# A two-layer trunk on one core: the upper half of x loaded by blocks and transposed on VectorE instead of TensorE

## The chip, the cores and the metric

The kernel runs on one core of a Trainium2 chip. The metric is the device time of one execution in microseconds; below, the median of three runs and the time of the one execution that was profiled. The core's engines take their instructions in the order in which the program lists them for each engine, and wait for each other by semaphores: TensorE (PE; its weight loads are PEld), VectorE (DVE), ScalarE (ACT), GpSimd (POOL) and SyncE (SP), which issues most of the transfers (DMAs).

## What is computed

Two pre-norm residual layers over 256 positions with 1024 channels, float32: attention with 8 heads of 128 and partial rotary in layer 0, a pooling mixer in layer 1, a squared-ReLU MLP of 4096 behind each, and a last norm. For this change only the front of layer 0 matters:

```python
def rms_norm(x, g):
    xf = x.astype(jnp.float32)
    y = xf * lax.rsqrt(jnp.mean(xf * xf, axis=-1, keepdims=True) + NORM_EPS)
    return (y * g.astype(jnp.float32)).astype(x.dtype)
...
    xn = rms_norm(x, norm_mix[i])
...
    qkv = (xn @ w_qkv).reshape(b, s, 3, N_HEADS, HEAD_DIM)
    q, k, v = [jnp.transpose(qkv[:, :, i], (0, 2, 1, 3)) for i in range(3)]
    q = apply_partial_rope(q, cos, sin)
    k = apply_partial_rope(k, cos, sin)
```

## The kernel before

Every product is a sum of three in a shorter float32 form (float32r): a value is cut into a high part and a low part, and high x high, high x low and low x high are added. For weights, `split_steps` makes the parts: ACT copies a raw slab into `wh` (line 169), then DVE subtracts and writes `wl` (line 173). A slab is 1 MB (128 partitions x 2048 columns). The first two slabs (`raw_v_0`, `raw_v_1`) are cut in four pieces of 512 columns, the others in two of 1024. `pump(n)` puts n such pieces into the program, high then low; `use` makes sure that the pieces needed next are in it. When the last low piece of a slab is in the program, the transfer of the slab three places later is issued on SP (`load_to`, `load`), since there are three raw buffers.

The activations need channels on partitions: x arrives with tokens on partitions (`xt`) and is turned. `transposes(k0, ...)` has PE transpose tile k0 (and its neighbour, n=2) of 128 channels against the identity into PSUM (`tr_a`, line 302); then `evac_h` (ACT, line 308) writes the high part into `xs[:, k, 0:256]`, multiplied by the norm's gain `gcol`, and `evac_l` (DVE, line 314) the low part. The norm's 1/rms is put on later, as a factor of the results.

The stage in question is the loop `for k in range(KT)` at line 471: per tile k of 128 channels, twelve products of 512 columns (line 485) add the tile's share to the four banks `d_v` of v = x w_v (two halves of tokens, two of columns). Slab `v_j` holds the weight rows of tiles 2j and 2j + 1. The dictionary `ahead` says in which step the transposes of later tiles stand. ACT also squares x here (`junk`, line 499), a quarter in each of the steps k = 2 to 5, for the mean square; after step 5 `avar` (DVE), `aerr` (ACT, a square root) and a row of small DVE operations make 1/rms and two diagonal matrices. Behind the loop come k and q of each pair of heads, channel tile by channel tile (`u_k`, `u_q`, lines 375 to 380).

The rotary angles are computed on POOL from `pos_i` and `inv` (`rotary`, lines 437 to 446); DVE takes the last turn (`last_turn`), ACT the sines, POOL the cosine, DVE the tables `ct` and `st`, which every q and k is multiplied with (`qk_evac`, line 557 on).

At the very front PE multiplies zeros (`keep_warm`): six products (N_WARM) before the first transposes, two (N_WARM2) behind them. The zeros are a tile `warm` that DVE sets. The order of all engines is the order of the code (a manual schedule).

Of the kernel before, what the change touches and what calls it, by code (L numbers as in the profile page):

```python
# [11 lines left out]
F32 = mybir.dt.float32  # L12
F32R = mybir.dt.float32r
I32 = mybir.dt.int32
AF = mybir.ActivationFunctionType
# [3 lines left out]
P = 128  # L19
SEQ = 256  # L20
D = 1024
# [18 lines left out]
W_BUFS = 5  # L40
AHEAD = 3
N_WARM = 6
N_WARM2 = 2

# [38 lines left out]
def tile_trunk(ctx: ExitStack, tc: tile.TileContext, x_in, positions, norm_mix, norm_mlp,  # L85
# [16 lines left out]
    def rows(ap, r0):  # L102
        return ap[r0:r0 + 2 * P, :].rearrange("(k p) f -> p k f", p=P)

    def cols(ap, c0):
        return ap[:, c0:c0 + 2 * P].rearrange("(k p) f -> p k f", p=P)

    wv = w_qkv[:, 2 * D:3 * D]
    for j in range(4):
        slabs.append((("v", j), rows(wv, 2 * P * j)))  # L110
    for j in range(4):
        slabs.append((("k", j), cols(w_qkv, D + 2 * P * j)))
        slabs.append((("q", j), cols(w_qkv, 2 * P * j)))
# [25 lines left out]
    def load(i):  # L139
        key, ap = slabs[i]  # L140
        if key[0] == "p":
            raws[i] = folded["w"]
            return None
        raw = rawp.tile([P, SLAB], F32, tag="raw", name="raw_%s_%d" % key)
        raws[i] = raw
        rv = raw.rearrange("p (k f) -> p k f", k=ap.shape[1])
        if i > 0:
            nc.sync.dma_start(rv, ap)
        return rv

# [74 lines left out]
        return (wh.rearrange("p (k f) -> p k f", k=kk), wl.rearrange("p (k f) -> p k f", k=kk))  # L225


    warm = cpool.tile([P, P], F32, name="warm")
    nc.vector.memset(warm, 0.0)
    ident = cpool.tile([P, P], F32, name="ident")  # L230
    make_identity(nc, ident)
    ones = cpool.tile([P, P], F32, name="ones")
# [7 lines left out]
    def load_x(k, n):  # L240
        cs = slice(k * P, (k + n) * P)
        nc.sync.dma_start(xt[:, :, cs], x_v[:, :, cs])
# [8 lines left out]
    load_x(0, 1)  # L251
    nc.scalar.dma_start(grow, norm_mix.rearrange("l (k p) -> (l k) p", p=P))
    pos_i = cpool.tile([ROT, SEQ], I32, name="pos_i")
    nc.scalar.dma_start(pos_i, positions.broadcast_to([ROT, SEQ]))
    inv_b = cpool.tile([ROT, P], F32, name="inv")
    nc.scalar.dma_start(inv_b, consts[0:ROT, C_INV:C_INV + P])
    inv = inv_b[:, 0:1]
    load_v0(nc.sync, 0, 0)
    load_v0(nc.sync, 0, 1)
    load_x(1, 1)  # L260
    nc.sync.dma_start(v0[:, 1, :], v0_src[:, 1, :])
    load_x(2, 2)
    raw1 = rawp.tile([P, SLAB], F32, tag="raw", name="raw_v_1")
    raws[1] = raw1
    state["raw"] = 2
    for k in range(2):
        nc.sync.dma_start(raw1[:, k * D:(k + 1) * D], slabs[1][1][:, k, :])
    tiny = cpool.tile([P, 96], F32, name="tiny")[:, 0:1]
    nc.scalar.activation(tiny, warm[:, 0:1], AF.Sqrt)
    load_x(4, 4)  # L270
    nc.sync.dma_start(grow2, norm_mlp.rearrange("l (k p) -> (l k) p", p=P))
    cst = cpool.tile([P, SLAB], F32, name="cst")[:, 0:C_ALL]
    load_to(RAW_BUFS - 1)

    xs = cpool.tile([P, KT, 2 * SEQ], F32R, name="xs")

# [16 lines left out]
    def transposes(k0, gbase, nm, dtag=None, n=2, t=None, tokens=range(NS)):  # L293


        if t is None and dtag:
            t = ps_d.tile([P, HALF], F32, tag=dtag, name="tr_%s_%d" % (nm, k0))
        elif t is None:
            t = ps_t.tile([P, HALF], F32, tag="t", name="tr_%s_%d" % (nm, k0))
        for a in range(n):  # L300
            for s in tokens:
                nc.tensor.transpose(t[:, a * SEQ + s * P:a * SEQ + (s + 1) * P],
                                    xt[:, s, (k0 + a) * P:(k0 + a + 1) * P], ident)

        def evac_h():
            for a in range(n):
                k = k0 + a
                nc.scalar.activation(xs[:, k, 0:SEQ], t[:, a * SEQ:(a + 1) * SEQ], AF.Copy,
                                     scale=gcol[:, gbase + k:gbase + k + 1])

        def evac_l():
            for a in range(n):
                k = k0 + a
                nc.vector.scalar_tensor_tensor(xs[:, k, SEQ:2 * SEQ], t[:, a * SEQ:(a + 1) * SEQ],
                                               gcol[:, gbase + k:gbase + k + 1],
                                               xs[:, k, 0:SEQ].bitcast(F32),
                                               op0=ALU.mult, op1=ALU.subtract)
        return evac_h, evac_l

    def both(pair):  # L320
        pair[0]()
        pair[1]()
# [145 lines left out]
    nc.vector.tensor_scalar(xs[:, 0, 0:SEQ], t0[:, 0:SEQ], gcol[:, 0:1], None, op0=ALU.mult)  # L468
    lo()
    pump_h(1)  # L470
    ahead = {0: (1, 1), 1: (2, 2), 3: (4, 2), 5: (6, 2)}
    for k in range(KT):
        wh, wl = use("v", k // 2, 99 if k % 2 else (2 if k < 4 else 1))
        ev = transposes(ahead[k][0], 0, "a", n=ahead[k][1]) if 0 < k and k in ahead else None
        steps = [(n, h) for n in range(3) for h in range(2)]
        if k == 0:
            steps.sort(key=lambda nh: nh[1])
        for n, h in steps:
            if k == 0 and (n, h) == (0, 1):
                both(transposes(1, 0, "a", n=1))  # L480
            hs = slice(h * HALF, (h + 1) * HALF)
            for s in range(NS):
                x0 = (SEQ if n == 1 else 0) + s * P
                w = wl if n == 2 else wh
                nc.tensor.matmul(dv[s, h], xs[:, k, x0:x0 + P], w[:, k % 2, hs],  # L485
                                 start=k == 0 and n == 0, stop=k == KT - 1 and n == 2)
        if k < 7:
            pump(2 if k < 3 else 1)
        if k == 2:
            load_to(3)  # L490
            nc.sync.dma_start(cst, consts[:, 0:C_ALL])
        if k == 6:
            gains(grow2, 16)
        if ev is not None:
            both(ev)
        if 2 <= k < 6:
            s, h = GR[k - 2]
            junk = work.tile([P, HALF], F32, tag="junk", name="junk", bufs=1)
            nc.scalar.activation(junk, xt[:, s, h * HALF:(h + 1) * HALF], AF.Square,
                                 scale=1.0 / 32.0, accum_out=acc0[:, h, s:s + 1])  # L500
        if k == 5:
            var0 = small.tile([P, NS], F32, tag="avar", name="avar", bufs=1)
            r0t = small.tile([P, NS], F32, tag="arst", name="arst", bufs=1)
            e0 = small.tile([P, NS], F32, tag="aerr", name="aerr", bufs=1)
            nc.vector.scalar_tensor_tensor(var0, acc0[:, 0, :], EPS, acc0[:, 1, :],
                                           op0=ALU.add, op1=ALU.add)
            nc.scalar.activation(e0, var0, AF.Sqrt)
            pump_h(1)
            nc.vector.reciprocal(r0t, e0)
            nc.vector.tensor_tensor(e0, var0, r0t, op=ALU.mult)  # L510
            nc.vector.tensor_tensor(e0, e0, r0t, op=ALU.mult)
            nc.vector.tensor_scalar(e0, e0, -0.5, 1.5, op0=ALU.mult, op1=ALU.add)
            nc.vector.tensor_tensor(r0t, r0t, e0, op=ALU.mult)
            r0 = [r0t[:, s:s + 1] for s in range(NS)]
            diags = []
            for s in range(NS):
                diag = small.tile([P, P], F32, tag="diag%d" % s, name="diag%d" % s, bufs=1)
                nc.vector.tensor_scalar(diag, ident, r0[s], None, op0=ALU.mult)
                diags.append(diag)
# [606 lines left out]
```

## Time and profile before

| | us |
|---|---|
| median of three runs | 485.59 (485.41 to 486.0) |
| the profiled execution, its own time | 485.4 |
| its span, first to last instruction | 483.4 |
| PE busy | 475.7 |
| DVE busy | 333.6 |
| ACT busy | 253.5 |
| POOL busy | 40.8 |

The span is what the engines' records cover; the time has 2.0 us more around it. The rows that are quoted from the timelines read: start in us from the span's start, busy us, engine, line, operation, what is written and read, number of instructions in a row, and in brackets the idle time of the engine ahead of it with what ended it. In the first 45 us the order of PE is: zeros, transposes, v (until 30.03), the first k (from 30.40), the first q (from 36.24), the second k (from 42.00).

### The profile page before, as it was taken

The numbers are of one execution on the slowest core, as the hardware profiler recorded it, in microseconds if no ns is written. First come the engines' busy times: TensorE is split into PE (matmuls) and PEld (weight loads), VectorE is DVE, ScalarE is ACT, GpSimd is POOL, SyncE is SP. The second block draws the span as 40 slices with busy tenths as digits, with TensorE's granted clock in tenths as the row PEclk, the third lists the DMA queues.
The fourth block names the chain that finished last, engine by engine and source line by source line (L and its number), as shares of the span: only waits on it lengthen the run. The fifth ranks groups of instructions, "written<-read, shape, count | busy, mean of one in ns | idle before, by whom it ended". The sixth has DMA issues, their size and how long they took to land.

```text
span 483.4 us, 6621 instructions
## 1 busy us (share of the span) xinstructions
PE 475.7 (98%) x2622; PEld 415.3 (86%) x2622; DVE 333.6 (69%) x492; ACT 253.5 (52%) x413; POOL 40.8 (8%) x38
## 2 busy tenths in 40 slices
PE   9999999999999999999999999999999999999994
PEld 7889999888888888888888889888888888888884
DVE  4789988855877484848566687678756557484745
ACT  5794655653686372635355554477535436272523
POOL 6920344300000000000000000000000000000000
PEclk9999999999999999999999999999999999999998
DMA  8975644480477757557574570078747472845202
GB/s 281 385 227 199 196 175 129 133 261 1 121 250 238 262 195 284 185 164 219 170 250 144 174 262 1 17 250 288 243 138 264 151 255 95 259 127 222 89 0 87
DMA packets 55982, 89.32 MB, mean 185 GB/s; under 512 B 1584, under 2 KB 44688, under 8 KB 55952
## 3 DMA queue, kind: packets, MB, share of 16 engines
q1 hardware_dynamic: 55536, 88.46, 55.3%
q10 hardware_dynamic: 416, 0.45, 0.3%
q8 instruction: 20, 0.33, 0.3%
q14 instruction: 10, 0.08, 0.0%
HBM read 87.85 MB, written 1.05 MB: 184 GB/s over the span
## 4 chain that ended last, share of the span: by engine, by line
PE 98%; DVE 0%; ACT 0%; issue 0%; ACTq 0%
PE u_m L397 24%; PE u_m L390 13%; PE d_m L366 12%; PE d_m L367 12%; PE d_m L368 12%; PE d_v L485 5%; PE u_q L380 2%; PE u_q L376 2%; PE u_k L376 2%; PE u_k L380 2%; PE u_k L375 2%; PE u_q L375 2%; PE d_o L366 2%; PE d_o L368 2%; PE d_o L367 2%; PE d_p L999 1%
## 5 line engine op out<-in xcount | busy, mean ns | idle before, releaser
L397 PE MATMUL u_m<-xs,wh_u 128*128 128x512 f32 x512 | 122.2, 390 | 0.0
L397 PEld LDWEIGHTS u_m<-xs,wh_u 128*128 128x128 f32 x512 | 94.7, 188 | 18.7
L366 PE MATMUL d_m<-wh_d,hh 128*128 128x512 f32 x252 | 98.1, 389 | 0.0
L368 PE MATMUL d_m<-wh_d,hl 128*128 128x512 f32 x252 | 98.0, 389 | 0.0
L367 PE MATMUL d_m<-wl_d,hh 128*128 128x512 f32 x252 | 98.0, 389 | 0.0
L173 DVE TENSOR_TENSOR wl_d<-raw_d,wh_d 128x1024 fp32r<-128x1024 f32 x64 | 76.2, 1221 | 17.6 <-ACT wh_d L169 17.6
L173 DVE TENSOR_TENSOR wl_u<-raw_u,wh_u 128x1024 fp32r<-128x1024 f32 x64 | 75.7, 1221 | 11.3 <-ACT wh_u L169 11.3
L169 ACT ACTIVATE wh_d<-raw_d 128x1024 fp32r<-128x1024 f32 x64 | 64.9, 1047 | 22.5 <-DMA raw_d<-in_mlp_w_down_dram 22.4
L733 ACT ACTIVATE t<-u_m 128x256 f32<-128x256 f32 x64 | 24.0, 378 | 83.1 <-PE u_m L390 54.5
L169 ACT ACTIVATE wh_u<-raw_u 128x1024 fp32r<-128x1024 f32 x64 | 63.9, 1045 | 6.2 <-DMA raw_u<-in_mlp_w_up_dram 6.2
L390 PEld LDWEIGHTS u_m<-xs,wl_u 128*128 128x128 f32 x512 | 64.1, 191 | 1.5
L390 PE MATMUL u_m<-xs,wl_u 128*128 128x256 f32 x512 | 65.3, 284 | 0.0
L734 DVE TENSOR_TENSOR t<-u_m,t 128x256 f32<-128x256 f32 x64 | 26.5, 422 | 53.7 <-ACT t L733 52.9
L368 PEld LDWEIGHTS d_m<-wh_d,hl 128*128 128x128 f32 x252 | 47.3, 188 | 9.8
L366 PEld LDWEIGHTS d_m<-wh_d,hh 128*128 128x128 f32 x252 | 47.3, 188 | 9.8
L367 PEld LDWEIGHTS d_m<-wl_d,hh 128*128 128x128 f32 x252 | 47.3, 188 | 9.8
L744 ACT ACTIVATE hh<-hf 128x512 fp32r<-128x512 f32 x32 | 20.2, 633 | 45.0 <-DVE hf L743 45.0
L745 DVE TENSOR_TENSOR hl<-hf,hh 128x512 fp32r<-128x512 f32 x32 | 22.2, 693 | 22.5 <-ACT hh L744 22.5
L743 DVE SCALAR_TENSOR_TENSOR hf<-t 128x512 f32<-128x512 f32 x32 | 22.2, 692 | 1.1
L375 PE MATMUL u_q<-xs,wh_q 128*128 128x256 f32 x64 | 18.7, 291 | 0.0
L375 PE MATMUL u_k<-xs,wh_k 128*128 128x256 f32 x64 | 18.5, 289 | 0.0
L380 PE MATMUL u_q<-xs,wh_q 128*128 128x256 f32 x64 | 18.1, 283 | 0.0
(205 smaller groups left out, 582.2 us busy)
## 6 DMA issues: line engine op xcount, KB each, us to landing
raw_u<-in_mlp_w_up_dram SPq DMA_DIRECT2D x32, 1024.0 KB, 6.4
raw_d<-in_mlp_w_down_dram SPq DMA_DIRECT2D x32, 1024.0 KB, 4.9
raw_k<-in_attn_w_qkv_dram SPq DMA_DIRECT2D x4, 1024.0 KB, 5.4
raw_q<-in_attn_w_qkv_dram SPq DMA_DIRECT2D x4, 1024.0 KB, 5.3
raw_o<-in_attn_w_o_dram SPq DMA_DIRECT2D x4, 1024.0 KB, 4.9
raw_v<-in_attn_w_qkv_dram SPq DMA_DIRECT2D x2, 1024.0 KB, 8.2
raw_v<-in_attn_w_qkv_dram SPq DMA_DIRECT2D x3, 512.0 KB, 6.5
pw<-in_pool_w_dram SPq DMA_DIRECT2D x1, 1024.0 KB, 9.2
```

The lines of the kernel that those rows point to most:

```text
L169: nc.scalar.activation(wh[:, sl], src[:, sl], AF.Copy)
L173: nc.vector.tensor_tensor(wl[:, sl], src[:, sl], wh[:, sl].bitcast(F32), op=ALU.subtract)
L366: nc.tensor.matmul(acc, lh, wh, start=first, stop=False)
L367: nc.tensor.matmul(acc, lh, wl, start=False, stop=False)
L368: nc.tensor.matmul(acc, ll, wh, start=False, stop=last)
L375: nc.tensor.matmul(o, w[0][:, k, fs], hi, start=first, stop=False, skip_group_check=True)
L380: nc.tensor.matmul(acc[:, f * SEQ:(f + 1) * SEQ], w[0][:, k, fs], xs[:, k, SEQ:2 * SEQ], start=False, stop=last, skip_group_check=True)
L390: nc.tensor.matmul(acc[:, 0:SEQ], w[1][:, k, f * P:(f + 1) * P], xs[:, k, 0:SEQ], start=first and k == 0, stop=not first and k == KT - 1, ...
L397: nc.tensor.matmul(acc, w[0][:, k, f * P:(f + 1) * P], xs[:, k, :], start=first and k == 0, stop=not first and k == KT - 1, skip_group_che ...
L485: nc.tensor.matmul(dv[s, h], xs[:, k, x0:x0 + P], w[:, k % 2, hs], start=k == 0 and n == 0, stop=k == KT - 1 and n == 2)
L733: nc.scalar.activation(t[:, ts], u[:, SEQ:2 * SEQ], AF.Copy)
L734: nc.vector.tensor_tensor(t[:, ts], u[:, 0:SEQ], t[:, ts], op=ALU.add)
```

## The change

x's channels 512 to 1023 get to `xs` in another way. Four DMAs load them a second time, in blocks: partition 32j + b of `xp` holds token b of each of the eight groups of 32 tokens, columns 128j to 128j + 127 of the upper half. `block_tile(k)` has DVE transpose 32x32 blocks of it (every fourth column), which gives a tile whose partition p is channel 512 + 4p + (k - 4); so the upper rows of all weights of q, k and v are loaded in that order (`upper`), and the gains `gx` too. The gain goes on in an ACT copy from SBUF and a DVE operation, as before from PSUM. The transposes of tiles 4 to 7 on PE are gone. `xt` still gets the upper half, for the squares and the residual, but later. Each k and q slab is loaded by two DMAs. The second row of v's first slab comes in two halves, and step 1 of the loop takes the columns' halves one after the other with the transposes of tiles 2 and 3 between them. `pos_i` and `inv` are loaded on SP's queue, behind `raw_v_1`, instead of ACT's. `warm` is a constant instead of a tile of its own, and N_WARM2 is 3.

```diff
-N_WARM2 = 2
+N_WARM2 = 3
...
+    def upper(ap):
+        return ap[HALF:D, :].rearrange("(p k) f -> p k f", k=4)
...
     for j in range(4):
-        slabs.append((("v", j), rows(wv, 2 * P * j)))
+        slabs.append((("v", j), rows(wv, 2 * P * j) if j < 2 else
+                      upper(wv)[:, 2 * j - 4:2 * j - 2, :]))
...
-        if i > 0:
+        if key[0] in ("k", "q"):
+            c0 = (D if key[0] == "k" else 0) + 2 * P * key[1]
+            nc.sync.dma_start(rv[:, 0:4, :], ap[:, 0:4, :])
+            nc.sync.dma_start(rv[:, 4:8, :], upper(w_qkv[:, c0:c0 + 2 * P]))
+        elif i > 0:
             nc.sync.dma_start(rv, ap)
...
-    warm = cpool.tile([P, P], F32, name="warm")
-    nc.vector.memset(warm, 0.0)
+    warm = nc.const_aps.tensor(0.0, (P, P), F32)
...
-    nc.scalar.dma_start(pos_i, positions.broadcast_to([ROT, SEQ]))
...
-    nc.scalar.dma_start(inv_b, consts[0:ROT, C_INV:C_INV + P])
...
-    nc.sync.dma_start(v0[:, 1, :], v0_src[:, 1, :])
+    load_v0(nc.sync, 1, 0)
+    load_v0(nc.sync, 1, 1)
...
+    nc.sync.dma_start(pos_i, positions.broadcast_to([ROT, SEQ]))
+    nc.sync.dma_start(inv_b, consts[0:ROT, C_INV:C_INV + P])
...
+    xp = cpool.tile([P, D], F32, tag="psb", name="xp")
+    xp_i = xp.rearrange("p (i c) -> p i c", i=8)
+    x_b = x_in.rearrange("(i b) (h j c) -> h j b i c", b=32, j=4, h=2)
+    for j in range(4):
+        nc.sync.dma_start(xp_i[32 * j:32 * j + 32], x_b[1, j])
+    gx = cpool.tile([P, 4], F32, name="gx")
+    nc.sync.dma_start(gx, norm_mix[0:1, HALF:D].rearrange("o (p k) -> (o p) k", k=4))
+    load_to(RAW_BUFS - 1)
     load_x(4, 4)
...
-    load_to(RAW_BUFS - 1)
...
+    def block_tile(k):
+
+        t = work.tile([P, SEQ], F32, tag="Y", name="xb_%d" % k, bufs=4)
+        nc.vector.transpose(t.rearrange("p (i b) -> p i b", b=32),
+                            xp.rearrange("p (i a k) -> p i a k", i=8, k=4)[:, :, :, k - 4])
+        g = gx[:, k - 4:k - 3]
+        nc.scalar.activation(xs[:, k, 0:SEQ], t, AF.Copy, scale=g)
+        nc.vector.scalar_tensor_tensor(xs[:, k, SEQ:2 * SEQ], t, g, xs[:, k, 0:SEQ].bitcast(F32),
+                                       op0=ALU.mult, op1=ALU.subtract)
...
-    ahead = {0: (1, 1), 1: (2, 2), 3: (4, 2), 5: (6, 2)}
+    ahead = {0: (1, 1), 1: (2, 2)}
     for k in range(KT):
         wh, wl = use("v", k // 2, 99 if k % 2 else (2 if k < 4 else 1))
-        ev = transposes(ahead[k][0], 0, "a", n=ahead[k][1]) if 0 < k and k in ahead else None
         steps = [(n, h) for n in range(3) for h in range(2)]
-        if k == 0:
+        if k < 2:
             steps.sort(key=lambda nh: nh[1])
         for n, h in steps:
-            if k == 0 and (n, h) == (0, 1):
-                both(transposes(1, 0, "a", n=1))
+            if k < 2 and (n, h) == (0, 1):
+                both(transposes(*ahead[k][:1], 0, "a", n=ahead[k][1]))
...
-        if ev is not None:
-            both(ev)
         if 2 <= k < 6:
+            block_tile(k + 2)
             s, h = GR[k - 2]
```

What stands where on the engines follows from the order of the code. On DVE, in the steps k = 1 to 5 of the v loop, there stood before (wl_v_j is a piece of slab j's low part, tr_a_4 the transposes of tiles 4 and 5 in PSUM):

```order
L173 TENSOR_TENSOR wl_v_1_209<-raw_v_1_105,wh_v_1_208 128x512 x2
L314 SCALAR_TENSOR_TENSOR xs_115<-tr_a_2_191,gcol_123,xs_115 128x256 x2
L173 TENSOR_TENSOR wl_v_1_209<-raw_v_1_105,wh_v_1_208 128x512 x2
L173 TENSOR_TENSOR wl_v_2_257<-raw_v_2_113,wh_v_2_256 128x1024
L314 SCALAR_TENSOR_TENSOR xs_115<-tr_a_4_239,gcol_123,xs_115 128x256 x2
L173 TENSOR_TENSOR wl_v_2_257<-raw_v_2_113,wh_v_2_256 128x1024
L173 TENSOR_TENSOR wl_v_3_302<-raw_v_3_189,wh_v_3_301 128x1024
L314 SCALAR_TENSOR_TENSOR xs_115<-tr_a_6_284,gcol_123,xs_115 128x256 x2
L505 SCALAR_TENSOR_TENSOR avar_311<-acc0_151 128x2
```

On DVE at the same place of the changed kernel (xb_4 to xb_7 are the transposed tiles):

```order
L331 SCALAR_TENSOR_TENSOR xs_121<-tr_a_2_204,gcol_129,xs_121 128x256 x2
L182 TENSOR_TENSOR wl_v_1_220<-raw_v_1_102,wh_v_1_219 128x512 x4
L340 STREAM_TRANSPOSE xb_4_245<-xp_109 128x256
L344 SCALAR_TENSOR_TENSOR xs_121<-xb_4_245,gx_114,xs_121 128x256
L182 TENSOR_TENSOR wl_v_2_264<-raw_v_2_116,wh_v_2_263 128x1024
L340 STREAM_TRANSPOSE xb_5_267<-xp_109 128x256
L344 SCALAR_TENSOR_TENSOR xs_121<-xb_5_267,gx_114,xs_121 128x256
L182 TENSOR_TENSOR wl_v_2_264<-raw_v_2_116,wh_v_2_263 128x1024
L340 STREAM_TRANSPOSE xb_6_290<-xp_109 128x256
```

Each transpose stands behind the low piece of the step before it; it goes on in this way to xb_7 and avar. On ACT, in the same steps, there stood before (junk is the square of a quarter of x):

```order
L169 ACTIVATE wh_v_2_256<-raw_v_2_113 128x1024
L308 ACTIVATE xs_115<-tr_a_4_239,gcol_123 128x256 x2
L499 ACTIVATE junk_264,acc0_151<-xt_90 128x512
L169 ACTIVATE wh_v_2_256<-raw_v_2_113 128x1024
L499 ACTIVATE junk_282,acc0_151<-xt_90 128x512
L169 ACTIVATE wh_v_3_301<-raw_v_3_189 128x1024
L308 ACTIVATE xs_115<-tr_a_6_284,gcol_123 128x256 x2
```

On ACT at the same place of the changed kernel:

```order
L178 ACTIVATE wh_v_1_219<-raw_v_1_102 128x512 x4
L343 ACTIVATE xs_121<-xb_4_245,gx_114 128x256
L524 ACTIVATE junk_249,acc0_157<-xt_88 128x512
L178 ACTIVATE wh_v_2_263<-raw_v_2_116 128x1024
L343 ACTIVATE xs_121<-xb_5_267,gx_114 128x256
L524 ACTIVATE junk_271,acc0_157<-xt_88 128x512
L178 ACTIVATE wh_v_2_263<-raw_v_2_116 128x1024
L343 ACTIVATE xs_121<-xb_6_290,gx_114 128x256
L524 ACTIVATE junk_294,acc0_157<-xt_88 128x512
L178 ACTIVATE wh_v_3_308<-raw_v_3_196 128x1024
```

The copies into xs, two in a row before, now stand one by one between the high pieces, and read what DVE transposed. On SP's queue, after the change, behind the first columns of x and v's first slab:

```order
L250 DMA xt_88<-in_x_dram 128x2x256
L274 DMA raw_v_1_102<-in_attn_w_qkv_dram 128x1024 x2
L275 DMA pos_i_94<-in_positions_dram 32x256
L276 DMA inv_95<-in_consts_dram 32x128
L284 DMA xp_109<-in_x_dram 32x8x128 x4
L286 DMA gx_114<-in_norm_mix_dram 128x4
L157 DMA raw_v_2_116<-in_attn_w_qkv_dram 128x2x1024
L250 DMA xt_88<-in_x_dram 128x2x512
```

Before, x's upper columns (128x2x512) and the second norm's gains stood between raw_v_1 and raw_v_2, and pos_i and inv on ACT's queue at the very start.

## The prediction

> **What bounds the kernel now.** I read the page first, then the timelines of PE, ACT and DVE over the first 45 us, which is all that the change touches. The page says that the end is set by PE alone:
>
> ```profile
> span 483.4 us, 6621 instructions
> PE 475.7 (98%) x2622; PEld 415.3 (86%) x2622; DVE 333.6 (69%) x492; ACT 253.5 (52%) x413; POOL 40.8 (8%) x38
> PE 98%; DVE 0%; ACT 0%; issue 0%; ACTq 0%
> ```
>
> The chain of waits is 98% PE, so a gap that opens in PE's row of products, or one that closes, goes into the time nearly in full. PE's timeline (start, us, what, count) gives the pace at the front, where the eight channel tiles k = 0 to 7 are multiplied with the v columns:
>
> ```profile
> 8.42 0.63 PE L485 MATMUL d_v<-wl_v,xs 128*128 128x512 f32 x2
> 9.10 0.63 PE L302 MATMUL tr_a<-ident,xt 128*128 128x128 f32 x4
> 9.48 2.08 PE L485 MATMUL d_v<-wh_v,xs 128*128 128x512 f32 x8
> 12.31 1.98 PE L485 MATMUL d_v<-wh_v,xs 128*128 128x512 f32 x8
> 15.04 0.60 PE L302 MATMUL tr_a<-ident,xt 128*128 128x128 f32 x4
> 15.39 2.10 PE L485 MATMUL d_v<-wh_v,xs 128*128 128x512 f32 x8
> 27.15 2.12 PE L485 MATMUL d_v<-wh_v,xs 128*128 128x512 f32 x8
> 30.40 0.36 PE L375 MATMUL u_k<-xs,wh_k 128*128 128x256 f32 x1
> 36.24 0.28 PE L375 MATMUL u_q<-xs,wh_q 128*128 128x256 f32 x1
> 42.00 0.28 PE L375 MATMUL u_k<-xs,wh_k 128*128 128x256 f32 x1
> ```
>
> One tile's twelve products take 15.04 - 12.31 = 2.73 us, 0.228 each. Whatever ACT and DVE must do per tile has to fit into 2.73 us, or PE waits. Tile 7 starts at 27.15, the first k product at 30.40.
>
> **What is removed.** Two groups of four transposes leave PE (tiles 4 and 5 at 15.04, tiles 6 and 7 later): 15.39 - 15.04 = 0.35 each, **-0.70 us** if PE stays the bound. The products of tile 0 end at 8.42 + 2 x 0.228 = 8.88, and PE waits until 9.10 for x's next columns. With row 1 of v's first slab in halves and the transposes of tiles 2 and 3 in the middle of tile 1, that 0.22 goes.
>
> **The product more at the front.**
>
> ```profile
> 4.60 1.06 PE L282 MATMUL warm_up<-warm 128*128 128x128 f32 x4
> 4.83 1.39 ACT L169 ACTIVATE wh_v<-raw_v 128x512 fp32r<-128x512 f32 x2 [1.15 <-DMA raw_v<-in_attn_w_qkv_dram]
> ```
>
> Two products (four rows) take some 0.9 us up to the first v product, one some 0.45. That first product needs wh's first half, ready about 4.83 + 0.70 = 5.53, so 0.45 more lies in a wait as long as PE's front starts earlier, which it may, since the zeros no longer wait for a memset on DVE. Bounds: -0.3 (PE reaches its full clock earlier) to +0.45 (no earlier start). I take 0.
>
> **What the moved transposes make: a loop.** The order of the changed kernel has DVE take, per tile, the low half wl of a v piece, then the block transpose T, then xs's low part; ACT takes the copy of T into xs, a square of x, then the next high half wh. So wh -> wl (needs wh) -> T (behind wl on DVE) -> copy (needs T) -> square -> next wh (behind both on ACT). Before, ACT's copies waited for PE, not for DVE. The prices, from ACT and from DVE:
>
> ```profile
> 10.21 1.15 ACT L169 ACTIVATE wh_v<-raw_v 128x512 fp32r<-128x512 f32 x2 [1.01 <-DMA raw_v<-in_attn_w_qkv_dram]
> 11.27 0.82 ACT L308 ACTIVATE xs<-tr_a,gcol 128x256 fp32r<-128x256 f32 x2
> 15.25 1.06 ACT L169 ACTIVATE wh_v<-raw_v 128x1024 fp32r<-128x1024 f32 x1 [1.52 <-DMA raw_v<-in_attn_w_qkv_dram]
> 16.22 0.82 ACT L308 ACTIVATE xs<-tr_a,gcol 128x256 fp32r<-128x256 f32 x2
> 16.93 0.63 ACT L499 ACTIVATE junk<-xt 128x512 f32<-128x512 f32 x1
> 17.45 0.20 ACT L499 ACTIVATION_READ_ACCUMULATOR junk<-xt 128x1 f32 x1
> 17.55 1.05 ACT L169 ACTIVATE wh_v<-raw_v 128x1024 fp32r<-128x1024 f32 x1
> 21.61 0.84 ACT L308 ACTIVATE xs<-tr_a,gcol 128x256 fp32r<-128x256 f32 x2 [1.45 <-PE tr_a L302]
> 23.58 0.21 ACT L507 ACTIVATE aerr<-avar 128x2 f32<-128x2 f32 x1 [0.53 <-DVE avar L505]
> 23.70 1.04 ACT L169 ACTIVATE wh_v<-raw_v 128x1024 fp32r<-128x1024 f32 x1
> ```
> ```profile
> L173 DVE TENSOR_TENSOR wl_v<-raw_v,wh_v 128x1024 fp32r<-128x1024 f32 x4 | 5.4, 1342 | 2.3 <-ACT wh_v L169 2.3
> L173 DVE TENSOR_TENSOR wl_v<-raw_v,wh_v 128x512 fp32r<-128x512 f32 x6 | 4.1, 725 | 0.9 <-ACT wh_v L169 0.9
> 23.27 0.28 DVE L505 SCALAR_TENSOR_TENSOR avar<-acc 128x2 f32<-128x2 f32 x1
> 28.09 1.22 DVE L173 TENSOR_TENSOR wl_k<-raw_k,wh_k 128x1024 fp32r<-128x1024 f32 x1
> 29.22 0.28 DVE L449 TENSOR_SCALAR rot_b<-rot_a 32x256 f32<-32x256 f32 x1
> 33.84 0.43 DVE L543 SCALAR_TENSOR_TENSOR ct_k<-rb,cos_t 128x256 f32<-128x256 f32 x1 [0.99 <-POOL cos_t L459]
> 34.84 0.40 DVE L544 SCALAR_TENSOR_TENSOR st_q<-rb,sin_t 32x256 f32<-32x256 f32 x1
> 36.52 0.01 DVE L557 LOAD_MASK_SELECT sw_k<-u_k  x1 [1.27 <-ACT vsb L530]
> 39.51 2.34 DVE L173 TENSOR_TENSOR wl_k<-raw_k,wh_k 128x1024 fp32r<-128x1024 f32 x2
> 44.06 0.73 DVE L557 STREAM_SHUFFLE sw_q<-u_q 32x512 f32<-32x512 f32 x1
> ```
>
> wh 1.05; hand-over 0.03 (avar ends at 23.55, aerr starts at 23.58); wl 1.34, of which its end overlaps 0.09 with what follows on DVE (28.09 + 1.22 against 29.22), so 1.25; T; hand-over 0.03; copy 0.36 (16.22 to 16.93 for two); square 0.62 (16.93 to 17.55). No transpose on DVE stands in this trace: its bounds are 0.28 (29.22, 256 columns of 32 partitions) and 0.73 (the shuffle, the one other operation here that moves data between partitions, at twice the columns). I take 0.43, the row at 33.84, which has its size. **Loop: 1.05 + 0.03 + 1.25 + 0.43 + 0.03 + 0.36 + 0.62 = 3.77 us, against PE's 2.73.** About 1 us per tile is lost once the lead is used up.
>
> [...] That both engines keep their order is what closes the loop: the row at 21.61 shows ACT idle for 1.45 us in front of a copy while the wh_v at 23.70 stood behind it. [...]
>
> **The sum.** Tile 1: half 0 from 8.88, six products, 10.25; four transposes, the last ends 0.63 later, 10.88. Then ACT: two copies from 10.91 to 11.62, and only now v's second slab in four pieces, 0.53 apart (10.21 to 11.27 for two), the first ready at 12.24. Tile 2 starts at 12.27, as before (12.31): the 0.22 above is given back here. DVE: four low pieces from 12.27, 3 x 0.635 + 0.725, end 14.90; T of tile 4 from 14.81 to 15.24; copy from 15.27, square from 15.63, wh for tile 4 from 16.25 to 17.30. PE wants tile 4 at 12.27 + 2 x 2.73 = 17.73: in time. Tile 5's wh is ready at 17.30 + 3.77 = 21.07, wanted at 20.46: 0.6 late. Tile 6: 24.84, wanted at 23.8: 1.0 late. For tile 7 the variance stands in the loop too: the square's last read (17.45 + 0.20 is 0.72 after 16.93) instead of 0.62, hand-over 0.03, avar 0.28, hand-over 0.03, aerr 0.12 to the next start: 0.56 more. So tile 7's wh is ready at 24.84 + 3.77 + 0.56 = 29.17, wanted at 27.6; tile 7 starts 2.0 us later than at 27.15.
>
> Behind it on DVE stands an unbroken row from the end of aerr (23.79) to the second low half of k's first slab (29.31): 5.52 us. PE had 1.1 us of slack there (30.40). aerr now ends at 29.17 - 1.04 + 0.09 = 28.22, the row at 33.74, and the first k product starts at 33.8 instead of 30.40: **+3.4 us**. PE alone would be ready at 29.2 + 3.25 = 32.45, so DVE comes last.
>
> After that the pieces keep step with PE: second low half of the next k slab at 41.85 (39.51 + 2.34), 0.15 before PE wants it at 42.00, and both move by 3.4. So nothing more is added and, with PE without a gap after, nothing is won back. The two DMAs in the place of one per k and q slab have the same bytes and rows of the same length; ACT reaches those slabs later than before.
>
> **The queues.** pos_i and inv go from ACT's queue, where they were early, behind v's second slab on SP:
>
> ```profile
> 4.62 0.39 POOL L437 CAST rot_a<-pos_i 32x256 f32<-32x256 int32 x1 [2.92 <-DMA pos_i<-in_positions_dram]
> 24.07 0.74 POOL L446 TENSOR_TENSOR rot_a<-rot_a,rot_b 32x256 f32<-32x256 f32 x1
> grow<-in_norm_mlp_dram SPq DMA_DIRECT2D x1, 8.0 KB, 7.3
> 10.00:15.00 5.00, 5.00 (x23) 4.08 (x22) 3.54 (x7) 3.53 (x8) 4.68 (x5) 1.00 1.04 418
> ```
>
> 8 KB that stood behind large loads took 7.3 us to land, so pos_i lands with the slab ahead of it: its first half is waited for until 10.21, the second is 512 KB at 418 GB/s later, 11.5. POOL's row takes 24.81 - 4.62 = 20.2 us, so it ends at 31.7. DVE wants it right after 33.74: covered, by the delay of the loop alone. x's blocks (xp, 512 KB) come next, at 12.7 to 13.5 (full rate to about half of it); T wants them at 14.81. v's third slab has the same bytes ahead of it as before (xp instead of x's upper columns): 15.25 to about 16, wanted at 16.25. If that cover fails, each us of lateness is one of the sum.
>
> **Total: profiled run 485.4 us (span 483.4, 2.0 around it), close to the median of 485.59; 485.4 + 3.4 = 488.8.** Its own range: T of 0.28 or 0.73 makes -0.6 or +1.2 (four in the path), wl of 1.22 -0.4, the front -0.3 or +0.4: 487.5 to 490.8.
>
> **Rivals.**
> - The loop fits (say T stands ready early, its input there since 13.5): then the edits give their 0.70, and 0.2 at the front: 484.5, **faster**. It needs wh, wl, T, copy and square in 2.73 us; wh and wl alone are 2.3, the copy and the square 0.98, so only a T that doesn't wait for wl would do it, and pos_i would have to be early too. 0.06.
> - POOL becomes the bound: with the loop hidden, DVE's last turn of the angles waits until 31.7 instead of 29.22, the tables end 2.5 later, at 37.7 instead of 35.24 (34.84 + 0.40), and the first rotation, begun at 36.52, begins 1.2 later, and with it the low halves that PE waits for at 42.00: 486.6. 0.08.
> - Loads: xp or the third slab lands 1 to 2 us after T or wh wants it, the loop starts that much later: 490 to 490.8. 0.09.
> - Gains and waits balance within 0.2% (1 us, about what a measurement here can tell from no change), with a short T and slack that I don't see: 485.5. 0.06.
> - The forecast, 0.71.
>
> The range 486.9 to 490.8 holds the forecast, the loads and a part of POOL. Faster 0.06, same 0.07, slower 0.87.
>
> **What would show it.** In the changed profile: idle time of ACT before the xs copy, ended by DVE's xb; idle time of DVE before wl_v, ended by ACT's wh_v; starts of wh_v's pieces 3.8 apart; PE gaps of 0.5 to 1.5 us before tiles 5, 6 and 7 and at the first u_k; u_k at about 33.8. The cast of pos_i at 11.5. The step is wrong if wh_v's pieces come under 3 us apart or PE shows no gap there; the rotary step is wrong if the cast is before 8; and a T far from 0.43 moves the sum by four times the difference.

## The result, and the profile after

The changed kernel takes 492.03 us (median of 4 runs, 491.64 to 492.34) against 485.6 us (4 runs, 485.41 to 486.0) for the kernel before on the same chip: a ratio of **1.0131, 95% interval 1.0117 to 1.0146**, 6.4 us slower. The forecast was 488.8 us with a range up to 490.8: the side was right, the size too small by 3.2 us. The head of the page of the profiled execution (span, busy time of each engine, chain of waits):

```profile
span 489.6 us, 6637 instructions
PE 476.1 (97%) x2616; PEld 413.8 (85%) x2616; DVE 337.1 (69%) x495; ACT 254.0 (52%) x413; POOL 40.1 (8%) x38
PE 91%; DMA 3%; DVE 2%; ACT 1%; SPq 1%; issue 0%; DVEq 0%; ACTq 0%
```

PE's busy time is nearly what it was (475.7 before). The span has grown by 6.2 us, and the chain of waits has pieces that stood at nothing before: DMA 3%, DVE 2%, ACT 1%, SP's queue 1%. PE's timeline shows where (start, us, what, count, and in brackets the idle time ahead with what ended it):

```profile
19.74 2.12 PE L511 MATMUL d_v<-wh_v,xs 128*128 128x512 f32 x8 [1.84 <-ACT wh_v L178]
23.64 2.12 PE L511 MATMUL d_v<-wh_v,xs 128*128 128x512 f32 x8 [0.86 <-ACT wh_v L178]
28.06 2.12 PE L511 MATMUL d_v<-wh_v,xs 128*128 128x512 f32 x8 [1.37 <-ACT wh_v L178]
33.05 2.14 PE L511 MATMUL d_v<-wh_v,xs 128*128 128x512 f32 x8 [1.78 <-ACT wh_v L178]
36.63 0.36 PE L402 MATMUL u_k<-xs,wh_k 128*128 128x256 f32 x1
```

Tiles 4, 5, 6 and 7 each wait for the high half of their weights, 1.84, 0.86, 1.37 and 1.78 us. The first k product starts at 36.63 where it started at 30.40: 6.2 us, the whole difference of the spans. Behind it the engines keep step (the first u_q 5.83 us later, 5.84 before), so all of the loss lies in the first 37 us.

What the high halves waited for, from ACT's timeline:

```profile
13.49 1.15 ACT L178 ACTIVATE wh_v<-raw_v 128x512 fp32r<-128x512 f32 x2 [0.90 <-DMA raw_v<-in_attn_w_qkv_dram]
18.63 1.06 ACT L178 ACTIVATE wh_v<-raw_v 128x1024 fp32r<-128x1024 f32 x1 [1.49 <-DMA raw_v<-in_attn_w_qkv_dram]
21.52 0.51 ACT L343 ACTIVATE xs<-xb,gx 128x256 fp32r<-128x256 f32 x1 [1.83 <-DVE xb L340]
22.55 1.04 ACT L178 ACTIVATE wh_v<-raw_v 128x1024 fp32r<-128x1024 f32 x1
26.97 1.04 ACT L178 ACTIVATE wh_v<-raw_v 128x1024 fp32r<-128x1024 f32 x1
31.96 1.04 ACT L178 ACTIVATE wh_v<-raw_v 128x1024 fp32r<-128x1024 f32 x1
```

The first row is the second half of v's second slab, which itself came late, at 13.5. The next, for tile 4, waited for v's third slab, which came in at 18.6. The other three have no wait of their own: ACT is idle ahead of the *copy* in front of them, until DVE has turned a tile (xb). They start 3.92, 4.42 and 4.99 us apart; PE needs 2.73 per tile. That is the loop of the forecast, and DVE and POOL show why it is longer than the 3.77 (4.33 for the last) that was worked out:

```profile
15.37 0.62 DVE L340 STREAM_TRANSPOSE xb<-xp 128x256 f32<-128x256 f32 x1
19.72 1.23 DVE L182 TENSOR_TENSOR wl_v<-raw_v,wh_v 128x1024 fp32r<-128x1024 f32 x1 [2.67 <-ACT wh_v L178]
20.86 0.62 DVE L340 STREAM_TRANSPOSE xb<-xp 128x256 f32<-128x256 f32 x1
23.62 1.73 DVE L182 TENSOR_TENSOR wl_v<-raw_v,wh_v 128x1024 fp32r<-128x1024 f32 x1 [0.86 <-ACT wh_v L178]
28.04 1.70 DVE L182 TENSOR_TENSOR wl_v<-raw_v,wh_v 128x1024 fp32r<-128x1024 f32 x1 [0.89 <-ACT wh_v L178]
35.11 1.22 DVE L182 TENSOR_TENSOR wl_k<-raw_k,wh_k 128x1024 fp32r<-128x1024 f32 x1
36.33 1.22 DVE L182 TENSOR_TENSOR wl_k<-raw_k,wh_k 128x1024 fp32r<-128x1024 f32 x1
37.46 0.27 DVE L476 TENSOR_SCALAR rot_b<-rot_a 32x256 f32<-32x256 f32 x1
```
```profile
13.72 0.39 POOL L464 CAST rot_a<-pos_i 32x256 f32<-32x256 int32 x1 [12.02 <-DMA pos_i<-in_positions_dram]
23.55 0.72 POOL L473 TENSOR_TENSOR rot_a<-rot_a,rot_b 32x256 f32<-32x256 f32 x1
24.36 1.70 POOL L472 TENSOR_SCALAR rot_b<-rot_b 32x256 f32<-32x256 f32 x1
32.33 0.72 POOL L473 TENSOR_TENSOR rot_a<-rot_a,rot_b 32x256 f32<-32x256 f32 x1
```

The block transpose takes 0.62. The low half wl takes 1.23 once and 1.73 and 1.70 in the next two turns. In those two a POOL operation had begun just before: one at 23.55, over at 24.27, and wl ends at 25.35, 1.08 after that; POOL's next one, begun at 24.36, takes 1.70 where its like at 31.35 takes 0.90. wl is 0.50 and 0.47 us longer there than at 19.72, and POOL's operation 0.80 longer than at 31.35; why was not shown. POOL's row of angles, which before ended at 24.8, now ends at 33.05 and so lies beside the whole loop.

Why the slab came late, from SP's timeline, its waits, and the table by stretches (from:to, length, busy us and instructions of PE, PEld, DVE, ACT, POOL, then granted clock, busy share of the DMA engines, GB/s). First the change:

```profile
10.69 0.35 SPq L286 DMA_DIRECT2D gx<-in_norm_mix_dram  x1
13.49 0.39 SPq L157 DMA_DIRECT2D raw_v<-in_attn_w_qkv_dram  x1
SPq L157 <- DMA raw_v<-in_attn_w_qkv_dram: 2.4, 1, 2.4
11.00:14.00 3.00, 2.95 (x13) 2.00 (x12) 2.08 (x4) 2.10 (x5) 0.28 (x1) 1.00 0.91 152
```

Then the kernel before (the row at 6.48 is the third slab's issue and the fourth's):

```profile
6.48 3.93 SPq L148 DMA_DIRECT2D raw_v<-in_attn_w_qkv_dram  x2
11.00:14.00 3.00, 3.00 (x15) 2.49 (x14) 3.00 (x6) 2.74 (x7) 2.83 (x3) 1.00 1.04 420
```

SP issued the third slab at 13.49, after 2.4 us of waiting for a piece of the *second* slab to land. The DMAs here report on eight semaphores in turn, and each waits for the one eight places ahead: in the change six issues in a row, the four of xp, gx and the third slab, come 0.02 us after that one's last report. By SP's and ACT's order of issue the third slab had been eight places behind the second piece of v's first slab and was issued at 6.48. With six DMAs added ahead of it (one piece more of v's first slab, four for xp, gx) and two moved behind it (x's upper columns, the second norm's gains) it is eight places behind the second half of v's second slab, which landed at 13.47 where it had landed at 11.42 before. In the meantime the DMA engines are 91% busy and move 152 GB/s, where the kernel before moved 420 in the same stretch. Over 3 us that is 0.80 MB less, 1.9 us at the old rate. Not all of it is slow packets: with quick ones, in the run with the blocks to all partitions below, the stretch still moves only 212 GB/s, since the third slab goes out at 11.94 there.

### The profile page after: what moved, and what is told of

The parts are those of the page before. It is cut to its first block, busy times and chain, and to the rows that moved or that the text cites. A ratio compares the mean times of both kernels' runs of the same rounds, so it can differ in the third digit from the quotient of the medians.

```text
span 489.6 us, 6637 instructions
## 1 busy us (share of the span) xinstructions
PE 476.1 (97%) x2616; PEld 413.8 (85%) x2616; DVE 337.1 (69%) x495; ACT 254.0 (52%) x413; POOL 40.1 (8%) x38
## 4 chain that ended last, share of the span: by engine, by line
PE 91%; DMA 3%; DVE 2%; ACT 1%; SPq 1%; issue 0%; DVEq 0%; ACTq 0%
PE u_m L424 24%; PE u_m L417 13%; PE d_m L393 12%; PE d_m L395 12%; PE d_m L394 12%; DMA raw_v<-in_attn_w_qkv_dram 3%; PE u_q L407 2%; PE u_k L407 2%; PE u_q L403 2%; PE u_k L403 2%; PE u_k L402 2%; PE u_q L402 2%; PE d_o L393 2%; PE d_o L395 1%; PE d_o L394 1%; DVE wl_v L182 1%
## 5 line engine op out<-in xcount | busy, mean ns | idle before, releaser
L182 DVE TENSOR_TENSOR wl_u<-raw_u,wh_u 128x1024 fp32r<-128x1024 f32 x64 | 75.7, 1221 | 11.5 <-ACT wh_u L178 11.5
L511 PE MATMUL d_v<-wh_v,xs 128*128 128x512 f32 x64 | 17.2, 406 | 6.3 <-ACT wh_v L178 5.8
L511 PEld LDWEIGHTS d_v<-wh_v,xs 128*128 128x128 f32 x64 | 11.3, 188 | 10.6 <-ACT wh_v L178 8.5
L402 PE MATMUL u_q<-xs,wh_q 128*128 128x256 f32 x64 | 18.7, 291 | 0.0
```

The costliest lines, as they stand in the source:

```text
L182: nc.vector.tensor_tensor(wl[:, sl], src[:, sl], wh[:, sl].bitcast(F32), op=ALU.subtract)
L402: nc.tensor.matmul(o, w[0][:, k, fs], hi, start=first, stop=False, skip_group_check=True)
```

## The experiments

Ten kernels ran. Ratios are against the kernel before on the same chip (485.84 us in the first two batches, 485.75 in the last). Times are medians. Where a run is set against the changed kernel, the two ran on chips whose times of the kernel before differ by up to 0.2 us.

**The front alone.** The kernel before with the zeros, the product more, row 1 of v's first slab in halves, and tile 1's order of the change:

```diff
-N_WARM2 = 2
+N_WARM2 = 3
...
-    nc.sync.dma_start(v0[:, 1, :], v0_src[:, 1, :])
+    load_v0(nc.sync, 1, 0)
+    load_v0(nc.sync, 1, 1)
...
-        if k == 0:
+        if k < 2:
             steps.sort(key=lambda nh: nh[1])
```

> The kernel before with the front of the change alone: constant zeros, one fill-up product more, row 1 of v's first slab in halves, step 1 by halves with the transposes of tiles 2 and 3 in its middle. By the prediction's sum these give nothing: 485.6 us, within 0.3. Rival (they are a gain that the rest of the change hides): up to 0.6 less, 485.0 us; or the later copies of tiles 2 and 3 cost: 486.

Measured: 485.32 us (10 runs), ratio 0.9993 [0.9983, 1.0002]. The front costs and brings nothing that can be told from no change.

**The late positions alone.** The kernel before, with pos_i and inv loaded behind `raw_v_1` on SP:

```diff
-    nc.scalar.dma_start(pos_i, positions.broadcast_to([ROT, SEQ]))
-    nc.scalar.dma_start(inv_b, consts[0:ROT, C_INV:C_INV + P])
...
+    nc.sync.dma_start(pos_i, positions.broadcast_to([ROT, SEQ]))
+    nc.sync.dma_start(inv_b, consts[0:ROT, C_INV:C_INV + P])
```

> The kernel before with pos_i and inv alone moved to the sync queue behind v's second slab. By the second rival of the prediction (angles late, tables late): cast at about 11.6 us, last turn near 31.8, second k product 1.2 us later, 486.8 us, 486.3 to 487.3. If the late angles are hidden: 485.6 us.

Measured: 487.29 us (5 runs), ratio 1.0035 [1.0021, 1.0050], +1.45 us. DVE's timeline has the wait that the forecast priced as a rival, in the first row (the second row's 0.99 stood there before, too):

```profile
32.96 0.28 DVE L449 TENSOR_SCALAR rot_b<-rot_a 32x256 f32<-32x256 f32 x1 [2.37 <-POOL rot_a L446]
37.58 0.42 DVE L543 SCALAR_TENSOR_TENSOR ct_k<-rb,cos_t 128x256 f32<-128x256 f32 x1 [0.99 <-POOL cos_t L459]
```

The last turn comes 3.7 us later than at 29.22, of which 1.45 reach the end. In the changed kernel the same turn (37.46 above) has no wait: there the loop covers it.

**All four turns first.** The changed kernel, with the four block transposes in a row in step 2, so that none stands behind a low half of v:

```diff
-    def block_tile(k):
+    xbs = {}
+    def block_turn(k):
         t = work.tile([P, SEQ], F32, tag="Y", name="xb_%d" % k, bufs=4)
+        xbs[k] = t
...
+    def block_tile(k):
+        t = xbs[k]
...
+        if k == 2:
+            for kk in range(4, KT):
+                block_turn(kk)
         if 2 <= k < 6:
```

> The changed kernel with the four block transposes in one row on VectorE in step 2; copies, squares and loads stay. Loop theory (ScalarE and VectorE wait for each other once per tile because each transpose stands behind a wl): the PE gaps before tiles 5, 6 and 7 (1.0, 1.5 and 1.8 us) go, the one before tile 4 (2.0) stays, tile 7 starts near 28.1 instead of 33.05; the late angles on GpSimd (done at 33.05) then take back about 1.2 us: 487.9 us, 487 to 489. Rival (the loads alone make tiles 4 to 7 late): the gaps stay, 491.5 to 492.5 us.

Measured: 489.62 us (9 runs, 486.39 to 490.16), ratio 1.0063 [1.0044, 1.0082]; 2.4 us less than the change. The loop is gone from the profiled execution (489.91 us, one of the longer ones): PE's timeline has no wait ahead of tiles 5 to 7, and only the slab's ahead of tile 4:

```profile
20.05 2.11 PE L518 MATMUL d_v<-wh_v,xs 128*128 128x512 f32 x8 [1.68 <-ACT wh_v L178]
22.90 1.98 PE L518 MATMUL d_v<-wh_v,xs 128*128 128x512 f32 x8
25.62 1.98 PE L518 MATMUL d_v<-wh_v,xs 128*128 128x512 f32 x8
31.92 0.36 PE L409 MATMUL u_k<-xs,wh_k 128*128 128x256 f32 x1
45.59 0.39 PE L410 MATMUL u_k<-xs,wl_k 128*128 128x256 f32 x1 [1.20 <-DVE wl_k L182]
```
```profile
15.93 2.19 DVE L343 STREAM_TRANSPOSE xb<-xp 128x256 f32<-128x256 f32 x4
35.84 0.28 DVE L483 TENSOR_SCALAR rot_b<-rot_a 32x256 f32<-32x256 f32 x1 [2.36 <-POOL rot_a L480]
```

The first k product is 1.5 us behind the 30.40 of before, but the span is 4.5 us longer: the late angles, no longer covered, hold DVE for 2.36 us, and PE waits for low halves of k later on. They take back 3.0 us, where 1.2 was expected. POOL's row of angles ends at 35.80 here, against 32.92 with the late positions alone: its cast began 1.8 us later, and the row took 1.1 us longer. Cutting one wait uncovered the other.

**The positions early again.** The changed kernel with pos_i and inv on ACT's queue, as before:

```diff
+    nc.scalar.dma_start(pos_i, positions.broadcast_to([ROT, SEQ]))
+    nc.scalar.dma_start(inv_b, consts[0:ROT, C_INV:C_INV + P])
...
-    nc.sync.dma_start(pos_i, positions.broadcast_to([ROT, SEQ]))
-    nc.sync.dma_start(inv_b, consts[0:ROT, C_INV:C_INV + P])
```

> The changed kernel with pos_i and inv loaded first on ScalarE's queue again. Queue theory (v's third slab is issued late because the transfer eight places ahead of it has to land first, and with two transfers fewer behind the second slab that one is an earlier one): the third slab is issued before 10 us instead of at 13.5, its first high half starts near 17.1 instead of 18.63, the loop stays: 490.0 us, 489.3 to 491. Rival (the slab is late because the blocks of x take long to land, whatever stands in the queue): 491.5 to 492.3 us. The cast of pos_i goes back to about 4.6 us; by the loop theory that alone gives nothing.

Measured: 489.26 us (4 runs), ratio 1.0074 [1.0056, 1.0092]; 2.8 us less than the change, though no wait for the angles had shown in it. ACT's high halves and one low half of DVE:

```profile
18.05 1.06 ACT L178 ACTIVATE wh_v<-raw_v 128x1024 fp32r<-128x1024 f32 x1 [0.35 <-DMA raw_v<-in_attn_w_qkv_dram]
21.97 1.04 ACT L178 ACTIVATE wh_v<-raw_v 128x1024 fp32r<-128x1024 f32 x1
25.87 1.04 ACT L178 ACTIVATE wh_v<-raw_v 128x1024 fp32r<-128x1024 f32 x1
30.20 1.04 ACT L178 ACTIVATE wh_v<-raw_v 128x1024 fp32r<-128x1024 f32 x1
26.94 1.23 DVE L182 TENSOR_TENSOR wl_v<-raw_v,wh_v 128x1024 fp32r<-128x1024 f32 x1 [1.08 <-ACT wh_v L178]
```

POOL is done at 22.7, every low half takes 1.23, and the loop is 3.92, 3.90 and 4.33. So 1.2 us of the change's loop (4.42 + 4.99 against 3.90 + 4.33) came from POOL's row beside it, and the third slab, issued at 9.71, came 0.6 earlier. The first k product is at 34.54.

**Both.** Turns first and positions early, with the two edits above in full:

```diff
+    nc.scalar.dma_start(pos_i, positions.broadcast_to([ROT, SEQ]))
...
+            for kk in range(4, KT):
+                block_turn(kk)
...
```

> The changed kernel with both: the four block transposes in a row in step 2, and pos_i and inv first on ScalarE's queue. If the loss is the loop, the late angles and the late third slab, and nothing else, only the last is left, the 1.0 us gap before tile 4, against the transposes saved: first k product near 30.8 (before: 30.40), 486.1 us, 485.6 to 486.7. Rival (something else in the changed loads or in the operations from SBUF costs as well): above 487.

Measured: 485.38 us (10 runs), ratio 0.9994 [0.9985, 1.0004]: **all of the loss is gone**, better than expected, and nothing is gained. One wait is left on PE:

```profile
18.76 2.11 PE L518 MATMUL d_v<-wh_v,xs 128*128 128x512 f32 x8 [0.59 <-ACT wh_v L178]
30.57 0.36 PE L409 MATMUL u_k<-xs,wh_k 128*128 128x256 f32 x1
```

**The blocks to all partitions.** In the changed kernel each of xp's four DMAs takes 128 columns to 128 partitions, in place of 32. xp then holds tokens on its partitions and not the blocks, so tiles 4 to 7 multiply other numbers; the operations and the bytes stay the same:

```diff
-    xp_i = xp.rearrange("p (i c) -> p i c", i=8)
+    xp_s = xp.rearrange("p (j s c) -> p j s c", j=4, s=2)
...
-        nc.sync.dma_start(xp_i[32 * j:32 * j + 32], x_b[1, j])
+        nc.sync.dma_start(xp_s[:, j], x_v[:, :, HALF + P * j:HALF + P * j + P])
```

> The changed kernel, but each of the four transfers of xp brings 128 columns of x's upper half to all 128 partitions instead of 256 tokens' blocks to 32: same bytes, same 512-byte packets, same count of transfers. It multiplies wrong values for tiles 4 to 7. If the narrow transfers are what delays the loads (512-byte packets took 27 ns at the start and some 50 here), v's second slab and with it the issue of the third come 1 to 1.5 us earlier, and the gap of 2.0 us before tile 4 shrinks to about 0.7; the loop stays: 490.7 us. If the place in the queue alone does it: 492.

Measured: 491.09 us (4 runs), ratio 1.0111 [1.0096, 1.0126], 0.9 us less than the change. In the records of the single packets, one of 512 bytes takes 27 ns here; in the change it takes 27 ns too, in the median, before 10.5 us, and 45 to 56 ns on the mean between 11 and 13 us. The DMA engines are 80% busy at 212 GB/s from 11 to 14 us, where the change had 91% at 152. SP issues the third slab 1.6 us earlier, and the high half for tile 4 starts 1.6 us earlier:

```profile
11.94 0.37 SPq L157 DMA_DIRECT2D raw_v<-in_attn_w_qkv_dram  x1
17.00 1.06 ACT L178 ACTIVATE wh_v<-raw_v 128x1024 fp32r<-128x1024 f32 x1 [0.17 <-DMA raw_v<-in_attn_w_qkv_dram]
33.50:36.50 3.00, 3.00 (x11) 2.33 (x10) 2.97 (x6) 2.97 (x5) 0.00 (x0) 0.51 0.50 163
```

So narrow transfers are a cost of their own here: into 32 partitions a packet took 1.7 to 2.1 times as long between 11 and 13 us. Why was not shown. The last row (a stretch of the table) tells why its profiled execution gained less at the first k product (36.49) than at tile 4: behind a wait of 1.78 us PE ran at a granted clock of 0.51 for some 3 us. The high halves start 4.18, 4.42 and 4.98 us apart: with quick loads and late positions the loop is as long as in the change, so it was POOL's row and not the loads that stretched it.

**The loop alone.** Positions early and the blocks to all partitions, so that neither POOL nor the loads matter, and the turns where the change has them. Tiles 4 to 7 again multiply other numbers:

```diff
+    nc.scalar.dma_start(pos_i, positions.broadcast_to([ROT, SEQ]))
...
+        nc.sync.dma_start(xp_s[:, j], x_v[:, :, HALF + P * j:HALF + P * j + P])
```

> The changed kernel with pos_i and inv early and xp loaded to all partitions as in the run before (wrong values in tiles 4 to 7): neither late loads nor GpSimd beside the loop, only the loop. By the prediction's sum with the measured transpose of 0.62: starts of v's high halves 3.9 us apart, no gap before tile 4, about 1 us each before tiles 5 and 6, 1.3 before 7: 488.3 us, 487.8 to 488.9. If loads were the real cause, near 486.

Measured: 488.88 us (4 runs), ratio 1.0067 [1.0052, 1.0082]. The high halves for tiles 4 to 7 start at 17.53, 21.44, 25.34 and 29.67; none waits for a load. On PE:

```profile
30.76 2.14 PE L511 MATMUL d_v<-wh_v,xs 128*128 128x512 f32 x8 [1.16 <-ACT wh_v L178]
34.01 0.36 PE L402 MATMUL u_k<-xs,wh_k 128*128 128x256 f32 x1
```

**Neither loop nor late loads.** The same, other numbers in tiles 4 to 7 included, with all four turns first:

```diff
+            for kk in range(4, KT):
+                block_turn(kk)
...
+        nc.sync.dma_start(xp_s[:, j], x_v[:, :, HALF + P * j:HALF + P * j + P])
```

> The transposes in a row in step 2, pos_i and inv early, xp to all partitions (wrong values in tiles 4 to 7): the change with all three causes taken out. By the prediction's first rival the saved 0.7 us on TensorE then shows: 485.1 us, 484.7 to 485.6. If it is above 486, a cause is missing.

Measured: 485.07 us (10 runs), ratio 0.9986 [0.9977, 0.9996]. Against the run before, only the place of the turns differs: 488.88 - 485.07 = **3.8 us is the price of the loop**. In the profiled executions the first k product moves by nearly as much, from 34.01 to 30.30:

```profile
30.30 0.36 PE L409 MATMUL u_k<-xs,wh_k 128*128 128x256 f32 x1
```

**Two tries at a faster one.** In the run with both edits the wait left ahead of tile 4 stood behind a square on ACT. First, the four squares one step later, and the row that makes 1/rms with them:

```diff
-            s, h = GR[k - 2]
+        if 3 <= k < 7:
+            s, h = GR[k - 3]
...
-        if k == 5:
+        if k == 6:
```

> The run with all four turns in a row and the positions loaded early (485.38 us, span 483.4), with ScalarE's four squares of x each issued one step later, so that the high half of tile 4's weights no longer stands behind a square (0.61 + 0.19 us there), and the row of the reciprocal one step later too. Theory: the one gap left in that run (0.75 us ahead of tile 4) was this square; without it the high half starts at about 17.0 in place of 17.67 and k's first product at about 29.95 in place of 30.57; time 484.8 us (484.4 to 485.3). Rival one: the high half waits for v's third slab or for the copy, which itself waits for VectorE's turns (15.99 to 18.18): the gap stays and the time is 485.4. Rival two: the gap goes, but the reciprocal's row and the rotary row on VectorE now end later and take it back by k's table, 485.4 or more.

Measured: 485.66 us (12 runs, 485.27 to 488.04), ratio 1.0002 [0.9993, 1.0011]: no gain. The profiled execution, 488.04 us, was the longest of the twelve; in it the third slab came in at 19.8, long after the copy ahead of tile 4's high half was done, so it shows what a late load costs but not what the other runs waited for. Which of the two rivals held is open.

Second, with this, the third slab issued ahead of xp:

```diff
+    load_to(RAW_BUFS - 1)
     tiny = cpool.tile([P, 96], F32, name="tiny")[:, 0:1]
...
-    load_to(RAW_BUFS - 1)
     load_x(4, 4)
```

> The same as the run with the squares later, and v's third slab issued on the sync engine's queue directly behind the second, ahead of the four transfers of x's upper half into 32 partitions each. Theory (the slab's wait for narrow transfers ahead of it is a cost of its own, and what is ahead in the queue sets what comes late): the slab lands 2 us or more before tile 4 wants it, and x's upper half lands later by the slab's megabyte, about 2.6 us at the 390 GB/s seen behind 15 us; the turns start at 16.5 to 18 in place of 15.99, so the copy and the low part for tile 4 come 0.5 to 2 us later and PE waits there instead: 485.4 us (484.8 to 486.5), not below the other. Rival: the narrow transfers are slow by their own packets, not by what is ahead, and land as before, so the time is that of the other run, 484.8.

Measured: 487.12 us (10 runs), ratio 1.0033 [1.0022, 1.0045], 1.5 us above the run with the squares later on the same chip, and outside the expected range. The slab is issued at 5.59 and nobody waits for it, but DVE's turns and ACT's copy now wait for xp, and PE 1.72 us for tile 4's weights behind that copy:

```profile
17.79 2.19 DVE L343 STREAM_TRANSPOSE xb<-xp 128x256 f32<-128x256 f32 x4 [1.75 <-DMA xp<-in_x_dram]
18.45 0.51 ACT L350 ACTIVATE xs<-xb,gx 128x256 fp32r<-128x256 f32 x1 [4.50 <-DVE xb L343]
```

Both loads are wanted at about 16 to 17 us, and in these two profiled executions whichever was issued second came late.

## Why the forecast was right in its side and wrong in its size

- **The loop** was right in its mechanism: the waits of ACT for xb, of DVE for wh_v, and PE's gaps ahead of tiles 5, 6 and 7 are there. With the turns first they vanish, and the loop's price by itself is 3.8 us.
- **Its terms were too small.** T was taken as 0.43 from the nearest row; it takes 0.62, inside the bounds of 0.28 and 0.73. Three turns of the loop hold it: +0.6. The wl of 1.25 was a little long (1.23 less the overlap of 0.09): -0.3. A copy by itself takes 0.42 and not half of a pair's 0.71: +0.2. The variance's row was 0.1 shorter than the 0.56 put in. So the run with early positions has 3.92, 3.90 and 4.33, 12.15 us in place of 11.87. Beside POOL the two later turns grew by 1.2 us more, most of it in wl (1.73 and 1.70). Together the three turns took 13.33 us, +1.46.
- **"v's third slab has the same bytes ahead of it as before", 15.25 to about 16, is the step that failed.** The bytes are the same. But xp's packets took up to twice as long, which held up the second slab as well, and there are more DMAs, so that the third slab's own issue waited for the second until 13.49. Its high half started at 18.63 in place of 16.25: +2.38. Of that 1.49 us is the wait for the slab in ACT's row; the rest is mostly T, which began at 15.37 in place of 14.81, behind the second slab's late half, and took 0.2 longer. The rival of late loads had this, at 1 to 2 us and a chance of 0.09, and was too small as well. That width costs is shown by the run with the blocks to all partitions; that the place in the queue decides which load comes late is shown by the run with the slab ahead. The two can be told apart by when the third slab had landed, by the records of its completion: at 18.61 in the change (issued at 13.49), at 18.03 with the positions early (issued at 9.71), at 16.98 with the blocks to all partitions (issued at 11.94), at 16.16 with both (issued at 9.46). The slow packets are worth 1.6 to 1.9 us, the later issue 0.6 to 0.8.
- **Both together are the miss up to tile 7**: 1.46 + 2.38 = 3.84, and its high half came at 31.96 in place of 28.13.
- **The step behind tile 7 was wrong the other way.** I let the first k product wait for the second low half of k's slab. It needs the first alone, done at 36.33; PE itself is what comes last, 36.63 - 33.05 = 3.58 after tile 7's start, where the forecast had 33.8 - 29.2 = 4.6. That gives back 1.0, and leaves 36.63 - 33.8 = 2.8 of lateness: the profiled execution took 491.64 us, 2.8 above the forecast, and the median is 0.4 above that. In the run of the loop alone the same error hides that tile 7 starts at 30.76 in place of 29.2: its k product, at 34.01, stands by chance beside the forecast 33.8.
- **The positions** were said to be covered. The last turn's wait is covered (37.46, no idle time ahead), though the cast came at 13.72 and not at 11.5. What was missed is that POOL's row then runs beside DVE's: 1.2 us of loop, and the row is uncovered as soon as the loop is mended (3.0 us with the turns first).
- **The shares, by the first k product**: it starts at 30.30 with none of the three causes, at 34.01 with the loop, at 34.54 with the narrow loads besides, and at 36.63 with the late positions as well. In this order the loop has 3.7 us, the narrow loads 0.5, and the late positions 2.1, through POOL's company and the later issue. Most of what the narrow loads put the slab off is hidden there, since with the loop alone ACT comes to the slab only at 17.53, 1.4 us after it landed.
- **The front at nothing** holds (0.9993, interval around 1). PE does get quicker sooner, as its bound of -0.3 has it: in the timelines its 128x128 rows start some 0.21 us apart until 5.24 before and until 4.30 in the change, and 0.11 apart later, the granted clock reading 1.00 all the while. But the first v product starts at 5.57, against 5.51 before, behind 0.41 us of idle time that DVE's xs ends.
- **The 0.70 us of PE transposes** fits: with neither loop nor late loads the time falls by 0.8 us (485.07 against 485.84; the interval allows 0.2 to 1.1), the most that any of these runs gained. Blocks in their right order and early positions bring 485.38, which is no gain that can be told.
- **Slips in the sum**: 488.8 + 1.2 + 0.4 is 490.4 and not 490.8; half the full rate would bring xp at 14.0 and not 13.5. Neither changes the account.

What stays open: how much of the smaller share, the later issue, is chance. Each landing is that of one execution, and the run with both edits and the run with the squares later, whose loads stand in the same order, landed the third slab at 17.40 and at 19.86. What made the second so much later was not found. Nor was it shown why xp's packets are slow between 11 and 13 us and not before.

## What to carry to other kernels

Work moved off the bound engine was free here only where the engines that took it over kept it off the path that feeds the bound one (485.07 us against 488.88): put a tile's preparation ahead of the step that needs it, not behind a product of the same step on an engine that keeps its order, as ACT did here, idle for 1.83 us ahead of a copy with the next high half behind it. Price a load by the length of its packets (27 ns, or 45 to 56) and by its place in the ring of completions (the third slab out at 9.71 or at 13.49), not by its bytes alone. A row of an idle engine that moves in time should be laid beside the other engines' rows at its new place, since its wait may be covered while its company is not (POOL's row: no wait at 37.46, 1.2 us of loop).

## What the runs showed of the hardware that was not expected

- A block transpose of 128x256 fp32 on DVE took 0.62 us, four in a row 2.19.
- An fp32 low half of 128x1024 on DVE took 1.22 to 1.23 us with POOL idle, 1.23 with a POOL operation of one input (32x256) begun 0.07 after it, and 1.70 to 1.73 with one of two such inputs begun 0.07 to 0.10 before it; POOL's next operation, of 0.90, took 1.70 there.
- 512-byte packets into 32 partitions, with four such transfers under way, took 45 to 56 ns on the mean between 11 and 13 us, into 128 partitions 27 ns; the 16 DMA engines showed 91% busy at 152 GB/s from 11 to 14 us.
- In the kernel before and the changed one the transfers of SP and ACT report on eight semaphores in turn, and none was issued before the one eight places ahead had landed: the third slab went out at 13.49, the second slab's half having landed at 13.47.
- After PE waits of 1.14, 1.37 and 1.78 us ahead of three tiles in a row, one profiled execution had a granted clock of 0.51 for 3 us (33.5 to 36.5); the changed kernel's own execution, with waits of 0.86, 1.37 and 1.78 there, had 1.00 from 33.5 to 36.5. What lowered it was not shown.
